# A two-layer network under a list scheduler: who takes a cast, four blocks to a value group, half-width levels

## The chip, the cores and the metric

The kernel runs on one core of a Trainium2 chip. The core has a matrix engine (TensorE, PE in the profile; its weight loads are listed apart as PEld), a vector engine (VectorE, DVE), a scalar engine (ScalarE, ACT), a general-purpose engine (GpSimd, POOL), and an engine that issues most of the DMA transfers here (SyncE, SP). The metric is device time in microseconds for one execution of the whole program.

## The reference

The reference is a small two-layer network in f32 over a sequence of 1024 tokens with width 1024. Layer 0 mixes tokens with sliding-window attention with sinks, layer 1 with a gated linear recurrence (HGRN2); each layer ends with an MLP with a squared ReLU. Cut to what matters:

```python
for layer in range(DEPTH):                       # DEPTH = 2
    h = rmsnorm(x, mix_norm[layer])
    if layer % 2 == 0:
        # 16 query heads, 4 key/value heads of 64, window 128, blocks of 128 tokens
        qkv = h @ w_qkv + b_qkv                   # rotary on q and k
        scores = einsum(q_block, [k_prev, k_own]) * HEAD_DIM ** -0.5   # masked to the window
        e = exp(scores - m); probs = e / (sum(e) + exp(sink - m))
        y = einsum(probs, [v_prev, v_own]) @ w_o
    else:
        q, f, i, g = split(h @ w_in, 4)           # 8 heads of 128, chunks of 64 tokens
        forget = lb + (1 - lb) * sigmoid(f); k = 1 - forget
        # per chunk, from the state and within the chunk with the decay between s and t
        o = (q * exp(b)) @ state + tril((q_t . decay(t, s) . k_s)) @ i
        y = (rmsnorm(o) * silu(g)) @ w_o
    x = x + y
    x = x + square(relu(rmsnorm(x) @ w_up)) @ w_down   # d_ff = 4096
return rmsnorm(x, final_norm)
```

## The kernel before

Activations are kept as tiles of 128 x 512 in f32. A large product is built from three products in the format fp32r, because one such product is not exact enough: each operand is split into a high part (a cast to fp32r) and a low part (the operand minus the high part). `mm3` issues high x high, high x low and low x high. `weight_split` makes the parts of a weight tile: `wh` is the high part, a cast, and `wl` the low part, a subtraction on DVE. `split` does the same to activations (tiles `a`, `t`). The MLPs go through a Strassen scheme with seven products, so sums of weights (`m`, `a`) are split too.

The stages follow one another and overlap at their seams. The first 80 us are the first half of the q, k, v projection; until about 290 the attention blocks run between the second half of it and the first half of the output projection; then the output projection ends (to 340). The first MLP's up projection takes 340 to 640, its down projection 640 to 930. From 960 to 1440 the recurrence runs for eight heads, with the projections of the gates between, and 1440 to 1545 is its output projection. The second MLP is 1545 to 1830 and 1830 to 2140.

**What sets the order.** Every operation is first recorded (`Net.op`, `copy`, `tt`, `mm`) with the engine or engines that can do it and an estimated cost; `Schedule.order` then makes a list schedule: it always serves the engine that is free first in its own estimate, and there takes the ready operation of the lowest rank. `issue` emits the operations in that order, so all instructions in the profile carry the line of its inner function, L333, and one has to go by the names of the tiles. Each engine runs its queue in this order on the chip.

Only one kind of operation has two engines to choose from: the casts that `copy` records with `("ACT", "DVE")`. When an engine would take such a cast, `better_elsewhere` asks whether the other engine, after what stands ahead there, would end it sooner; if so the engine leaves it and takes another. The recorded cost of a cast is lower on DVE than on ACT; recorded costs only steer the order.

**Attention.** `attend` handles, for each half of the sequence (four blocks of 128 tokens) and each key/value head, the blocks in turn. `attend_block` makes the scores (two PSUM buffers of the kind `q`), the masked softmax in an `m` tile, the transposed probabilities (one more `q` buffer) and two `t` tiles with what the values are multiplied by. After every two blocks `values` multiplies them in the column form of PE, which puts two products of 64 output rows beside one another in the array, into one `q` buffer, and copies the result out. There are four `q` and four `p` buffers of PSUM, 18 `t` tiles and 60 `a` tiles.

**Recurrence.** Inside a chunk of 64 tokens the scores are built in levels, so that the decay between two tokens can be put into the two factors. For level `lg` with half width H = 2^lg all 64 x 64 scores of all chunks are computed (16 products of 64 output rows in the column form, two records each in the trace), and a masked copy (`copy_predicated`) takes from them those where the later token is in the second half of a block of 2H and the earlier one in the first. Level -1 is the diagonal, and a last product covers pairs of chunks.

Of the kernel before, what the change touches and what calls it, by code (L numbers as in the profile page):

```python
# [17 lines left out]
P = 128  # L18
# [4 lines left out]
TH = T // NH  # L23
# [8 lines left out]
HD = 64  # L32
ROT = 16
NBLK = T // P
BPH = NBLK // NH
# [6 lines left out]
CH = 64  # L42
# [88 lines left out]
    "Pool": {"SP": 200.0, "PE": 190.0, "ACT": 75.0, "DVE": 74.0, "Pool": 102.0},  # L131
}
WEIGH = 1.0
DRAIN = {"whole": 120.0, "columns": 120.0}
LEAD = 100
WARM = 8
# [4 lines left out]
class Schedule:  # L141
# [42 lines left out]
    def order(self):  # L184
        free_at, pending, ready, done, form = {}, {}, {}, [], None
# [25 lines left out]
        def better_elsewhere(op, e, t):  # L211
            waiting = sum(o.ways[e][1] for _, o in ready[e] if not o.engine and len(o.ways) == 1)
            for other, (_, cost) in op.ways.items():
                if other != e:
                    ahead = sum(o.ways[other][1] for r, o in ready.get(other, ()) if r < op.rank and not o.engine)
                    if max(t, free_at.get(other, 0.0)) + ahead + cost < t + op.ways[e][1] + WEIGH * waiting:
                        return True
            return False

        while True:  # L220
            best = None
            for e in ENGINES:
                p, r = pending.setdefault(e, []), ready.setdefault(e, [])
                t = free_at.get(e, 0.0)
# [4 lines left out]
                if not r:  # L229
                    if not p:  # L230
                        continue
                    t = max(t, p[0][0])
# [4 lines left out]
            t, e = best  # L237
            p, r = pending[e], ready[e]
            while p and p[0][0] <= t:
                _, rank, op = heapq.heappop(p)  # L240
                heapq.heappush(r, (rank, op))
            left, op = [], None
            while r and op is None:
                rank, o = heapq.heappop(r)
                if o.engine:
                    continue
                if len(o.ways) > 1 and better_elsewhere(o, e, t):
                    left.append((rank, o))
                else:
                    op = o  # L250
# [6 lines left out]
            if op.form and op.form != form:  # L257
                form, t = op.form, t + DRAIN[op.form]
            free_at[e] = t + cost
# [19 lines left out]
class Net:  # L279
# [635 lines left out]
    def attend(self, hf, out):  # L915

        blocks = range(hf * BPH, hf * BPH + BPH)
        for gp in range(NG // 2):
            stacks = [[None] * 4 for _ in range(2)]
            for j in range(4):  # L920
                pq = self.psum("q")
                for n in blocks:
                    c = slice((n % BPH) * P, (n % BPH) * P + P)
                    self.transpose(pq[:, c], self.q[n][gp][:, j * P : j * P + P])
                for e in range(2):
                    r, o = self.rows(e)
                    s = self.a(F32R)
                    self.act(s[r], pq[r], AF.Copy, scale=HD**-0.5)
                    self.stt(s[o], pq[r], HD**-0.5, s[r].bitcast(F32), ALU.mult, ALU.subtract)
                    stacks[e][j] = s  # L930
            for e in range(2):
                g = 2 * gp + e
                for j in range(2):
                    out[g, j] = self.a()
                for n in blocks[::2]:
                    parts = []
                    for b in (n, n + 1):
                        parts.append(self.attend_block(g, b, stacks[e]))
                        yield
                    self.values(g, n, parts, out)  # L940

    def values(self, g, n, parts, out):

        tok = slice((n % BPH) * P, (n % BPH) * P + 2 * P)
        both = [y for block in parts for y, v in block]
        po = self.psum("q").rearrange("p (h s) -> p h s", h=2)
        for b, block in enumerate(parts):
            for k, (y, v) in enumerate(block):
                for rr in range(2):
                    self.mm(po[rr * HD : rr * HD + HD, :, b * P : b * P + P], v, y[:, 2 * rr : 2 * rr + 2],  # L950
                            k == 0, k == len(block) - 1, 2 * P, 2.0, "columns", both)
        for j in range(2):
            self.copy(out[g, j][:, tok].only(n), po[:, j], 2 * P)

    def attend_block(self, g, n, stacks):
        i = (n >= 3) + (n >= 6)
# [184 lines left out]
    def recurrence(self, e, gates, totals, out):  # L1141

        nc = self.nc
        NC = NH * BPH
        chunk = lambda z, j: z[:, j * CH : j * CH + CH]
        scores = self.t(F32, (P, NC, CH))
        tots, tot = [self.t(tag="m") for _ in range(NH)], [g[1] for g in gates]
        at = 0
        for lg in range(-1, LEVELS):
            part = self.psum("q").rearrange("p (c t) -> p c t", c=NC)  # L1150
            both = [z for q, f, k, g, v in gates for z in (q, k)]
            for hf, (q, f, k, g, v) in enumerate(gates):
                for c in range(BPH):
                    for b in range(2):
                        rows = slice(b * CH, b * CH + CH)
                        j = 2 * c + b
                        self.mm(part[rows, hf * BPH + c], chunk(k, j), chunk(q, j), True, True, CH, 2.06, "columns", both)
            if lg < 0:
                mask = self.diag.unsqueeze(1).to_broadcast([P, NC, CH])
                self.tt("DVE", scores, part, mask, ALU.mult)  # L1160
                for q, f, k, g, v in gates:
                    self.tt("any", q, q, f, ALU.mult)
                yield
                continue
            mask = self.level_mask[lg].unsqueeze(1).to_broadcast([P, NC, CH])
            self.op("DVE", nc.vector.copy_predicated, [scores], [mask, part], 70 + TH * 1.04, scores, mask, part)
            at, tot = self.double(1 << lg, gates, tot, tots, at)
            yield
        cross = self.psum("q")[:CH].rearrange("p (c t) -> p c t", c=NC)
        both = [z for q, f, k, g, v in gates for z in (q, k)]  # L1170
# [4 lines left out]
        for hf in range(NH):  # L1175
            s, c = self.t(F32, (P, BPH, 2, CH)), slice(hf * BPH, hf * BPH + BPH)
# [9 lines left out]
        for hf, (q, f, k, g, v) in enumerate(gates):  # L1186
            s = weights[hf]
# [34 lines left out]
            y = self.split(g, self.t if keep else None)  # L1222
# [169 lines left out]
```

## Time and profile before

| | |
|---|---|
| runs | 2169.42, 2171.11, 2174.44 us (median 2171.11) |
| the profiled execution | 2174.92 us, of which the span from first to last instruction is 2173.1 |
| mean granted clock of PE | 0.994 |
| busy: PE, DVE, ACT, POOL | 2136.3, 1818.1, 848.0, 61.2 us |
| DMA | 316.50 MB, mean 146 GB/s |

PE's products of 128 x 512 are its common unit; in the up projection of the first MLP 1307 PE records take 300 us. Busy times by stage:

| stretch (us) | what runs | PE | DVE | ACT |
|---|---|---|---|---|
| 0 to 80 | q, k, v, first half | 76.79 | 67.63 | 41.38 |
| 80 to 160 | attention | 76.39 | 70.71 | 50.66 |
| 160 to 240 | attention | 79.40 | 71.47 | 58.13 |
| 240 to 292 | end of attention | 47.45 | 48.66 | 44.89 |
| 640 to 930 | first MLP, down | 288.39 | 254.09 | 112.00 |
| 960 to 1060 | first gates | 98.85 | 94.10 | 50.65 |
| 1060 to 1440 | recurrence | 378.41 | 333.71 | 131.01 |
| 1830 to 2140 | second MLP, down | 307.12 | 269.92 | 124.08 |

How the rows of the profile are read: a row of the timeline has its start and its duration in us, the engine, the operation with output<-inputs (buffer numbers left out), its shape, the count of instructions drawn together, and in brackets how long the engine had stood idle before it and what ended that. A row of the waits has the waiting engine and tile, what it waited for, the sum in us, the number of times and the longest. A row of the table of stretches has the stretch, its length, the busy time of PE, PEld, DVE, ACT and POOL with counts, PE's granted clock, the share of DMA and GB/s. A row of groups has the count of instructions, their busy time in us, the mean of one in ns, and the engine's idle time before them with what ended most of it.

### The profile page before, as it was taken

The page shows a single profiled execution, that of the slowest core. Times are in us where ns is not written, and L with a number is a line of the kernel's source. Part 1 is how long each engine was busy: PE and PEld are TensorE (multiplying, and loading weights), DVE is VectorE, ACT ScalarE, POOL GpSimd, SP SyncE. Part 2 cuts the span into 40 slices and gives each one's busy share as a digit, 9 for nine tenths or more (in the row PEclk, how much of TensorE's full clock was granted, in tenths as well). Part 3 has the DMA queues.
Part 4 walks back from the last instruction along what each step waited for, and adds up shares of the span by engine and source line. Part 5 has one row for each costly group of instructions (what it writes and reads, how often), then busy time and mean ns, then how long its engine had stood idle before and what let it go on. Part 6 is the DMA issues. An engine that isn't in the chain of part 4 may idle for free.

```text
span 2173.1 us, 32411 instructions
## 1 busy us (share of the span) xinstructions
PE 2136.3 (98%) x11464; PEld 1723.3 (79%) x11464; DVE 1818.1 (84%) x3544; ACT 848.0 (39%) x1778; POOL 61.2 (3%) x121
## 2 busy tenths in 40 slices
PE   9999999999999999999999999999999999999998
PEld 7777778888887888877788888778788887888787
DVE  8899889767779888899998988878876678988886
ACT  5567755122134224465333333343421223422444
POOL 4030000000000000000100000000000000000000
PEclk9999999999999999999999999999999999999999
DMA  6212353333369767731111111547333336976652
GB/s 207 76 44 87 118 193 112 105 104 116 103 213 309 261 210 233 250 126 54 59 58 56 59 55 59 193 148 221 98 112 107 107 113 219 304 250 218 209 180 78
DMA packets 174274, 316.50 MB, mean 146 GB/s; under 512 B 19616, under 2 KB 21664, under 8 KB 174112
## 3 DMA queue, kind: packets, MB, share of 16 engines
q1 hardware_dynamic: 174112, 314.43, 44.7%
q8 instruction: 90, 1.47, 0.3%
q14 instruction: 72, 0.59, 0.1%
HBM read 250.39 MB, written 63.96 MB: 145 GB/s over the span
## 4 chain that ended last, share of the span: by engine, by line
PE 86%; DVE 7%; ACT 3%; issue 2%; DMA 2%; SPq 0%; POOL 0%; POOLq 0%; DVEq 0%; ACTq 0%
PE q L333 48%; PE p L333 38%; DVE a L333 3%; DVE t L333 2%; ACT a L333 1%; DVE wl L333 1%; DMA wr<-in_down 1%; DVE m L333 1%; ACT t L333 1%; DMA wr<-in_wqkv 0%; ACT wh L333 0%; ACT m L333 0%; DMA a<-in_x 0%; DVE wh L333 0%; SPq L333 0%
## 5 line engine op out<-in xcount | busy, mean ns | idle before, releaser
L333 PE MATMUL q<-a,wh 128*128 128x512 f32 x2560 | 799.9, 395 | 8.1 <-DVE t L333 3.4
L333 PE MATMUL p<-a,wh 128*128 128x512 f32 x2336 | 754.0, 401 | 6.1 <-ACT wh L333 3.4
L333 PEld LDWEIGHTS q<-a,wh 128*128 128x128 f32 x2560 | 481.1, 188 | 122.6 <-ACT t L333 4.3
L333 PEld LDWEIGHTS p<-a,wh 128*128 128x128 f32 x2336 | 431.7, 189 | 105.3 <-ACT wh L333 4.3
L333 PE MATMUL q<-a,wl 128*128 128x512 f32 x1280 | 500.3, 394 | 0.0
L333 PE MATMUL p<-a,wl 128*128 128x512 f32 x1168 | 462.3, 396 | 0.1
L333 PEld LDWEIGHTS q<-a,wl 128*128 128x128 f32 x1280 | 240.9, 188 | 56.9
L333 PEld LDWEIGHTS p<-a,wl 128*128 128x128 f32 x1168 | 220.3, 189 | 49.7 <-DVE wl L333 0.6
L333 DVE TENSOR_TENSOR wl<-wr,wh 128x512 fp32r<-128x512 f32 x352 | 240.9, 686 | 14.4 <-ACT wh L333 4.2
L333 ACT COPY t<-q 128x512 f32<-128x512 f32 (+2 forms) x201 | 111.7, 562 | 361.8 <-PE q L333 353.1
L333 DVE TENSOR_TENSOR a<-t,a 128x512 fp32r<-128x512 f32 (+1 forms) x294 | 194.7, 685 | 0.5 <-DMA t<-d 0.2
L333 DVE TENSOR_TENSOR wl<-m,wh 128x512 fp32r<-128x512 f32 x256 | 176.4, 690 | 15.5 <-ACT wh L333 6.7
L333 DVE CAST wh<-wr 128x512 fp32r<-128x512 f32 x202 | 86.2, 427 | 120.7 <-PE p L333 74.1
L333 ACT CAST wh<-m 128x512 fp32r<-128x512 f32 x154 | 95.9, 623 | 217.1 <-PE q L333 149.9
L333 DVE TENSOR_TENSOR t<-t,t 128x512 f32<-128x512 f32 (+3 forms) x265 | 157.5, 612 | 21.2 <-DMA t<-d 14.2
L333 ACT CAST a<-t 128x512 fp32r<-128x512 f32 x191 | 115.5, 618 | 127.0 <-PE q L333 82.5
L333 ACT CAST wh<-wr 128x512 fp32r<-128x512 f32 x150 | 92.7, 619 | 178.5 <-PE p L333 113.1
L333 DVE TENSOR_TENSOR m<-wr,wr 128x512 f32<-128x512 f32 x160 | 109.6, 688 | 24.9 <-DMA wr<-in_up 12.1
L333 PE MATMUL p<-wh,a 128*128 128x512 f32 x384 | 128.2, 402 | 0.9 <-ACT wh L333 0.7
L333 PEld LDWEIGHTS q<-t,t 128*64 128x64 f32 (+1 forms) x2160 | 98.0, 144 | 25.1 <-PE p L333 12.4
L333 PE MATMUL q<-t,t 128*64 128x64 f32 (+1 forms) x2160 | 112.8, 231 | 0.0
L333 DVE CAST wh<-m 128x512 fp32r<-128x512 f32 x102 | 43.9, 430 | 74.4 <-PE q L333 61.4
(118 smaller groups left out, 2133.5 us busy)
## 6 DMA issues: line engine op xcount, KB each, us to landing
t<-d SPq DMA_DIRECT2D x296, 256.0 KB, 4.6
wr<-in_down SPq DMA_DIRECT2D x256, 256.0 KB, 4.0
d<-t SPq DMA_DIRECT2D x180, 256.0 KB, 2.6
wr<-in_up SPq DMA_DIRECT2D x128, 256.0 KB, 3.0
wr<-in_win SPq DMA_DIRECT2D x68, 256.0 KB, 2.9
a<-d SPq DMA_DIRECT2D x60, 256.0 KB, 4.5
wr<-in_wqkv SPq DMA_DIRECT2D x48, 256.0 KB, 3.0
d<-a SPq DMA_DIRECT2D x48, 256.0 KB, 2.6
```

Of the source, the lines that this page charges most:

```text
L333: fn(*[place(a) for a in args], **{k: place(v) for k, v in kw.items()})
```

## The change

Three things are edited.

- `better_elsewhere` adds `SPARE` = 1000 ns to DVE's side of the comparison. DVE takes a cast only if ACT would end it more than 1 us later than DVE could.
- `attend` collects four blocks instead of two before it calls `values`, which now fills two `q` buffers in one stay in the column form. There are 8 such groups instead of 16; the products and the copies are the same in number and size.
- In `recurrence` the levels from 0 up compute only the columns of the later halves: `later` picks the second half of each block of 2H, so a product has 32 moving columns instead of 64, and the masked copy works on 256 elements for each partition instead of 512, with source, mask and target picked with strides. Level -1 and the last product stay.

```diff
+SPARE = 1000.0
...
-                    if max(t, free_at.get(other, 0.0)) + ahead + cost < t + op.ways[e][1] + WEIGH * waiting:
+                    spare = SPARE if e == "DVE" else 0.0
+                    if max(t, free_at.get(other, 0.0)) + ahead + cost < t + op.ways[e][1] + WEIGH * waiting + spare:
                         return True
...
-                for n in blocks[::2]:
+                for n in blocks[::4]:
                     parts = []
-                    for b in (n, n + 1):
+                    for b in range(n, n + 4):
                         parts.append(self.attend_block(g, b, stacks[e]))
                         yield
                     self.values(g, n, parts, out)
...
-        po = self.psum("q").rearrange("p (h s) -> p h s", h=2)
+        po = [self.psum("q").rearrange("p (h s) -> p h s", h=2) for _ in range(2)]
...
-                    self.mm(po[rr * HD : rr * HD + HD, :, b * P : b * P + P], v, y[:, 2 * rr : 2 * rr + 2],
+                    self.mm(po[b // 2][rr * HD : rr * HD + HD, :, b % 2 * P : b % 2 * P + P], v, y[:, 2 * rr : 2 * rr + 2],
                             k == 0, k == len(block) - 1, 2 * P, 2.0, "columns", both)
-        for j in range(2):
-            self.copy(out[g, j][:, tok].only(n), po[:, j], 2 * P)
+        for b in range(2):
+            for j in range(2):
+                self.copy(out[g, j][:, b * 2 * P : b * 2 * P + 2 * P].only(n + 2 * b), po[b][:, j], 2 * P)
...
-            part = self.psum("q").rearrange("p (c t) -> p c t", c=NC)
+            H = 1 << max(lg, 0)
+            n, width = (1, CH) if lg < 0 else (CH // (2 * H), CH // 2)
+            part = self.psum("q")[:, : NC * width].rearrange("p (c t) -> p c t", c=NC)
+            later = lambda z: z if lg < 0 else z.rearrange("p (n a h) -> p n a h", a=2, h=H)[:, :, 1]
...
-                        self.mm(part[rows, hf * BPH + c], chunk(k, j), chunk(q, j), True, True, CH, 2.06, "columns", both)
+                        self.mm(part[rows, hf * BPH + c], chunk(k, j), later(chunk(q, j)), True, True, CH, 2.06, "columns", both)
...
-            mask = self.level_mask[lg].unsqueeze(1).to_broadcast([P, NC, CH])
-            self.op("DVE", nc.vector.copy_predicated, [scores], [mask, part], 70 + TH * 1.04, scores, mask, part)
+            mask = later(self.level_mask[lg]).unsqueeze(1).to_broadcast([P, NC, n, H])
+            target = scores.rearrange("p c (n a h) -> p c n a h", a=2, h=H)[:, :, :, 1]
+            part = part.rearrange("p c (n h) -> p c n h", n=n)
+            self.op("DVE", nc.vector.copy_predicated, [target], [mask, part], 70 + NC * width * 1.04, target, mask, part)
```

Since all operations go through the list schedule, the edit moves instructions in the whole program. Of the 379 casts that DVE had it keeps 19, and ACT has 1034 instead of 674. Three places follow, each with an engine's rows before and after. A name has the tile's number and, behind the underscore, the value's number; the second differs between the two programs.

The first is ACT at the end of the first MLP's down projection, where the output of the MLP is normalized and the first weights for the next stage are split. Before:

```order
L333 ACTIVATE t2491_9696<-a2245_8785 128x512
L333 CAST wh2401_9702<-a1744_7052 128x512
L333 CAST wh2413_9706<-a1776_7171 128x512
L333 CAST wh2419_9710<-a1792_7229 128x512
L333 CAST a2482_9712<-t2481_9471 128x512
L333 ACTIVATE t2492_9716<-a2247_8795 128x512
L333 CAST wh2395_9720<-a1728_6988 128x512
L333 ACTIVATE t2532_9740<-a2129_8453,c01_91 128x512
```

After:

```order
L335 CAST a2437_9539<-a1840_7411 128x512
L335 ACTIVATE t2485_9543<-a2349_9170 128x512
L335 ACTIVATE t2457_9551<-a2351_9176,c01_91 128x512
L335 ACTIVATE t2486_9557<-a2351_9176 128x512
L335 CAST wh2395_9564<-a1728_6990 128x512
L335 CAST a2439_9573<-t2435_9159 128x512
L335 CAST a2445_9579<-t2441_9225 128x512
L335 ACTIVATE t2461_9584<-a2353_9182,c01_91 128x512
```

The high part wh2395 now stands directly behind the activation t2486, a square of a residual tile. Before, t2486 stands at row 698 of ACT's queue and wh2395 at row 725, behind wh2401, wh2413 and wh2419.

The second is ACT at the end of the recurrence's output projection, where the squares of the residual (t3716 to t3722) and the high parts of normalized input tiles stand between the casts of weights. Before:

```order
L333 ACTIVATE t3720_15968<-a3638_15778 128x512
L333 ACTIVATE t3721_15974<-a3648_15836 128x512
L333 ACTIVATE t3722_15977<-a3658_15907 128x512
L333 CAST wh3780_15980<-wr3772_15756 128x512
L333 CAST a3707_15983<-t3706_15848 128x512
L333 CAST a3710_15989<-t3709_15858 128x512
L333 CAST a3713_15993<-t3712_15869 128x512
L333 CAST a3685_15997<-t3684_15913 128x512
L333 COPY t3760_16001<-q3757_15885 128x512
L333 COPY t3761_16003<-q3758_15946 128x512
```

After:

```order
L335 ACTIVATE t3720_15961<-a3638_15775 128x512
L335 CAST a3701_15967<-t3671_15676 128x512
L335 ACTIVATE t3721_15971<-a3648_15834 128x512
L335 ACTIVATE t3722_15977<-a3658_15899 128x512
L335 CAST a3704_15981<-t3703_15788 128x512
L335 CAST wh3780_15984<-wr3772_15748 128x512
L335 COPY t3760_15988<-q3757_15883 128x512
L335 CAST a3699_15993<-t3667_15619 128x512
L335 CAST a3707_15999<-t3706_15845 128x512
L335 COPY t3761_16003<-q3758_15944 128x512
```

The copy t3760, which empties a PSUM buffer, moved directly behind wh3780; before, four casts of activations stand between. Ahead of wh3780 there are more casts than before (wh3755 and a3701, a3704 among the squares).

The third is DVE at the start of the first MLP's down projection, between the scaled squares t1603 and t1607 of the activation function; t1607 reads a PSUM buffer and thereby sets it free, and a1687 is a sum of activations that ACT casts next. Before:

```order
L333 SCALAR_TENSOR_TENSOR t1603_6731<-t1599_6686 128x512
L333 TENSOR_TENSOR m1673_6736<-wr1674_6692,wr1675_6702 128x512
L333 TENSOR_TENSOR a1686_6742<-t1682_6598,a1685_6654 128x512
L333 TENSOR_TENSOR a1680_6754<-m1673_6736,wr1665_6671 128x512
L333 TENSOR_TENSOR t1598_6646<-t1598_6646,t1600_6752 128x512
L333 TENSOR_TENSOR wl1645_6769<-m1641_6540,wh1644_6746 128x512
L333 SCALAR_TENSOR_TENSOR t1605_6776<-t1598_6646 128x512
L333 TENSOR_TENSOR a1687_6782<-t1688_6609,t1682_6598 128x512
L333 TENSOR_TENSOR a1702_6787<-t1698_6621,a1701_6668 128x512
L333 TENSOR_TENSOR a1703_6797<-t1704_6629,t1698_6621 128x512
L333 TENSOR_TENSOR a1695_6807<-a1687_6782,a1694_6792 128x512
L333 SCALAR_TENSOR_TENSOR t1607_6805<-q1594_6509,t1607_6805 128x512
```

After:

```order
L335 SCALAR_TENSOR_TENSOR t1603_6733<-t1599_6686 128x512
L335 TENSOR_TENSOR a1664_6740<-m1657_6706,wr1649_6562 128x512
L335 TENSOR_TENSOR a1687_6746<-t1688_6607,t1682_6595 128x512
L335 TENSOR_TENSOR a1702_6756<-t1698_6616,a1701_6670 128x512
L335 TENSOR_TENSOR t1598_6650<-t1598_6650,t1600_6754 128x512
L335 TENSOR_TENSOR wl1645_6773<-m1641_6547,wh1644_6763 128x512
L335 SCALAR_TENSOR_TENSOR t1605_6778<-t1598_6650 128x512
L335 TENSOR_TENSOR m1673_6784<-wr1674_6720,wr1675_6730 128x512
L335 TENSOR_TENSOR a1695_6791<-a1687_6746,a1694_6768 128x512
L335 TENSOR_TENSOR a1680_6797<-m1673_6784,wr1665_6668 128x512
L335 TENSOR_TENSOR a1703_6807<-t1704_6626,t1698_6616 128x512
L335 SCALAR_TENSOR_TENSOR t1607_6805<-q1594_6507,t1607_6805 128x512
```

The sum a1687 moved from seven rows behind t1603 to two; the weight sum m1673 moved behind t1605. Ten rows stand between t1603 and t1607 in both.

More of the change, by code (lines that the diff above doesn't have):

```diff
@@ L942, in values @@
     def values(self, g, n, parts, out):
-        tok = slice((n % BPH) * P, (n % BPH) * P + 2 * P)
         both = [y for block in parts for y, v in block]
-        po = self.psum("q").rearrange("p (h s) -> p h s", h=2)
+        po = [self.psum("q").rearrange("p (h s) -> p h s", h=2) for _ in range(2)]
         for b, block in enumerate(parts):
```

## The prediction

> **What bounds the kernel now.** I read the page's first part, then the table of stretches, then PE's waits, then the timeline around each of the longer ones.
>
> ```profile
> PE 2136.3 (98%) x11464; PEld 1723.3 (79%) x11464; DVE 1818.1 (84%) x3544; ACT 848.0 (39%) x1778; POOL 61.2 (3%) x121
> ...
> 240.00:292.00 52.00, 47.45 (x288) 35.38 (x289) 48.66 (x97) 44.89 (x135) 0.45 (x2) 0.97 0.54 176
> 340.00:640.00 300.00, 299.96 (x1307) 243.10 (x1306) 222.26 (x379) 72.92 (x131) 0.00 (x0) 1.00 0.38 119
> 930.00:960.00 30.00, 26.76 (x114) 21.48 (x113) 26.87 (x75) 16.90 (x32) 0.36 (x2) 0.94 0.38 117
> 1440.00:1545.00 105.00, 99.94 (x438) 80.71 (x437) 92.33 (x172) 50.90 (x90) 0.00 (x0) 0.95 0.58 184
> ```
>
> PE is busy 98% of the span, and in the first up projection (340:640) it has no gap at all, with DVE at 74% and ACT at 24%; the second reads the same. There nothing that is moved between DVE and ACT can shorten the kernel. What is left is 2173.1 - 2136.3 = 36.8 us in which PE stands still, and the time that a lowered clock costs: (1 - clock) x length is 1.6 us in 240:292, 1.8 in 930:960, 5.2 in 1440:1545. These three seams between stages are also where DVE is busiest (94%, 90%, 88%). Who keeps PE waiting:
>
> ```profile
> PE q L333 <- DVE t L333: 5.2, 6, 1.7
> PE q L333 <- DVE m L333: 5.0, 6, 3.2
> PE q L333 <- ACT t L333: 4.9, 5, 1.8
> PE p L333 <- ACT wh L333: 4.1, 3, 3.2
> PE q L333 <- DVE a L333: 2.4, 4, 1.6
> ```
>
> These five make 21.6 us, in 24 waits. So the prize of a better order is some 22 us plus slow clock, and the change must be priced wait by wait.
>
> **The casts.** The new rule leaves 19 of 379 casts on DVE and sends 360 to ACT.
>
> ```profile
> L333 DVE CAST wh<-wr 128x512 fp32r<-128x512 f32 x202 | 86.2, 427 | 120.7 <-PE p L333 74.1
> L333 DVE CAST wh<-m 128x512 fp32r<-128x512 f32 x102 | 43.9, 430 | 74.4 <-PE q L333 61.4
> L333 ACT CAST wh<-wr 128x512 fp32r<-128x512 f32 x150 | 92.7, 619 | 178.5 <-PE p L333 113.1
> ```
>
> Each takes about 0.43 us from DVE and 0.62 us on ACT: DVE loses 360 x 0.427 = 154 us (84% to 77%), ACT gains 223 us (39% to 49%). The idle time ahead of these casts on both engines was ended mostly by PE (it gives buffers back), so in the steady stages the cast waits for PE and not the reverse. The 0.19 us by which a cast gets longer is covered by that lead, and I cost it at nothing there, as I do the gain. If that cover were gone, every pair of MLP weights would pay; the rows at 340:640 with ACT at 24% say it has room. The casts therefore count only at the seams, below.
>
> **The masked copies.**
>
> ```profile
> L333 DVE COPY_PREDICATED t<-c,q 128x512 f32<-128x512 int32 x48 | 35.2, 734 | 9.2 <-PE q L333 8.3
> L333 DVE COPY_PREDICATED m<-c,q 128x256 f32<-128x256 int32 x56 | 23.7, 444 | 0.2
> ```
>
> 48 copies over half the elements: 48 x (0.734 - 0.444) = 13.9 us of DVE, in the recurrence, where PE is the bound. On the path: nothing. The new source and target are strided, which no row shows; bounds for one copy are 0.44 and the old 0.73 us, and either is hidden.
>
> **The halved level products.** 48 groups of 16 products, 32 records each, go from 64 to 32 moving columns.
>
> ```profile
> 998.99 0.95 PE L333 MATMUL q<-c,t 128*128 128x1 f32 x8
> 1004.88 1.05 PE L333 MATMUL q<-c,c 128*128 128x128 f32 x8
> 1073.70 1.15 PE L333 MATMUL q<-t,t 128*64 128x64 f32 x32
> ```
>
> The first two rows decide: eight products with one moving column take 0.95 us, eight with 128 take 1.05. With 128 times fewer columns the series loses 0.10 us, which is the end of its last product; the step between products is set by the load of the weights. The level's weights stay 64 columns wide, so its step should stay, and only the tail shrinks: 0.10 x 32/128 = 0.025 us, x 48 = 1.2 us. If the moving columns set the step after all (the series of 32 in 1.15 us would fall to half at best), the gain is 48 x 0.57 = 27 us; that is the upper bound and a rival. I take -1.2, nearest the one-column row. The Trainium skill has a rule for each: "TensorE: Matmul & The Clock Gate", section Back-to-back issue gap, makes the gap grow with the moving columns over 2.4 GHz, which is the gain; its section LDWEIGHTS makes a load cost its columns over 1.2 GHz, an estimated 53 ns for 64, which is none. The two rows side with the second.
>
> **The value groups.** Sixteen become eight, so PE enters and leaves the column form eight times less.
>
> ```profile
> 277.90 0.40 PE L333 MATMUL p<-a,wl 128*128 128x512 f32 x1
> 278.23 1.95 PE L333 MATMUL q<-t,a 128*64 128x256 f32 x16
> ```
>
> The group begins 0.33 us after a product that elsewhere is followed in 0.23 us (340:640 has 1307 records in 300 us), so entering costs 0.10 us; leaving I put at the same. 8 x 0.2 = -1.6 us; between 0.8 and 1.6. What the larger groups hold longer is under the rivals.
>
> **The seams, one by one.**
>
> Start. The first weight cast goes from DVE to ACT, into the queue that also scales the inputs.
>
> ```profile
> 4.27 0.63 DVE L333 CAST wh<-wr 128x512 fp32r<-128x512 f32 x1 [2.80 <-DMA wr<-in_wqkv]
> 4.43 0.72 ACT L333 ACTIVATE a<-a,c 128x512 fp32r<-128x512 f32 x1 [0.34 <-DMA c<-in_par]
> 5.21 0.80 PE L333 MATMUL p<-wh,a 128*128 128x512 f32 x1 [0.22 <-ACT a L333]
> 9.77 0.49 PE L333 MATMUL p<-wh,a 128*128 128x512 f32 x1 [0.65 <-ACT wh L333]
> ```
>
> Behind that activation and two small ones the cast ends near 5.9, not 4.9: the first product moves from 5.21 to about 6.1. The second set of weights (9.77) is cast behind one more input's two activations and comes about 1.8 later, but then finds its low half ready. Between +0.9 and +2.5, taken +1.2, near the first.
>
> End of attention.
>
> ```profile
> 285.18 0.63 PE L333 MATMUL q<-c,m 128*128 128x128 f32 x4 [3.23 <-DVE m L333]
> 286.45 3.26 PE L333 MATMUL q<-t,a 128*64 128x256 f32 x16
> 290.24 0.53 PE L333 MATMUL p<-a,wh 128*128 128x512 f32 x1 [0.53 <-DVE a L333]
> ```
>
> PE waits 3.2 us for a softmax block on DVE, and the value group behind it runs at the slow clock (3.26 us against 1.95): 3.23 + 1.31 + 0.53 = 5.1 us. In the new order DVE does the output projection's low halves far earlier, ahead of the last blocks, so PE has other products there, and four-odd us of casts are off DVE. But the softmax chain itself runs some blocks later. From 0 to -5.1, I take -3.
>
> Two waits of the down projections, of one kind.
>
> ```profile
> 654.85 0.73 PE L333 MATMUL q<-a,wh 128*128 128x512 f32 x2 [1.61 <-DVE t L333]
> 1847.56 0.73 PE L333 MATMUL q<-a,wh 128*128 128x512 f32 x2 [1.74 <-DVE t L333]
> ...
> 2023.50 0.73 PE L333 MATMUL q<-a,wh 128*128 128x512 f32 x2 [1.14 <-ACT t L333]
> 652.42 0.62 ACT L333 CAST a<-a 128x512 fp32r<-128x512 f32 x1 [1.62 <-DVE a L333]
> ```
>
> PE waits for DVE to read a PSUM buffer, DVE for a relu on ACT, and ACT stood 1.62 us in front of a cast of a DVE sum. In the new order that sum is five rows nearer to t1603 on DVE, 5 x 0.6 us, which more than ends ACT's wait; but then DVE's own ten rows set the time. About half goes: -0.8 each, -1.6 (0 to -3.3). At 2023.50 the copy that releases PE no longer stands behind a cast: -1.1 (0 to -1.1).
>
> Into the recurrence.
>
> ```profile
> 937.82 0.60 ACT L333 CAST wh<-a 128x512 fp32r<-128x512 f32 x1
> 938.48 1.76 PE L333 MATMUL p<-a,wh 128*128 128x512 f32 x4 [3.24 <-ACT wh L333]
> 950.00:960.00 10.00, 10.00 (x50) 8.29 (x49) 6.87 (x16) 2.07 (x4) 0.00 (x0) 1.00 0.61 206
> 965.00:990.00 25.00, 24.40 (x108) 18.91 (x107) 24.96 (x42) 19.39 (x36) 0.00 (x0) 1.00 0.08 31
> ```
>
> PE waits 3.24 us for wh2395 and then loses 1.8 us to the clock. The cast is needed first of its set and stands last; before, it stood 27 rows behind the activation t2486, in the new order it stands right behind it, and this wait goes. Late next is DVE: from 965 to 990 it is full, and PE, 5 us earlier, would catch up with it. What DVE can make good is its idle time, 10.00 - 6.87 = 3.1 us in 950:960. So -3 of 5 (0 to -5).
>
> Small waits in the recurrence.
>
> ```profile
> 1066.49 0.49 PE L333 MATMUL q<-t,m 128*128 128x128 f32 x2 [0.57 <-DVE m L333]
> ```
>
> Two or three like this one; DVE casts that stood ahead of what PE waits for are gone: -1 (0 to -1.5).
>
> Into the second MLP.
>
> ```profile
> 1530.64 0.60 ACT L333 CAST wh<-wr 128x512 fp32r<-128x512 f32 x1
> 1533.23 1.05 ACT L333 COPY t<-q 128x512 f32<-128x512 f32 x2
> 1531.30 0.73 PE L333 MATMUL q<-a,wh 128*128 128x512 f32 x2 [1.74 <-ACT wh L333]
> 1533.86 1.22 PE L333 MATMUL q<-a,wh 128*128 128x512 f32 x2 [1.83 <-ACT t L333]
> ```
>
> Two waits, 1.74 for wh3780 and 1.83 for a copy behind four more casts, then slow clock. In the new order two or three more ACT rows stand ahead of wh3780 (+0.9), and the copy follows it at once (the second wait gone, -1.8; clock up to -2.3). -2, between +0.9 and -3.2. The clock is the uncertain part: here 1.74 and 1.83 us of standing, with three products between, set off the slow stretch. The Trainium skill, "TensorE: Matmul & The Clock Gate", section What's actually happening, says a window of 3.4 us judged idle halves the clock; by it one wait of 2.6 us could escape or not, an estimated 2 us either way.
>
> New waits. ACT is at 44.89 of 52 us in 240:292 and now takes nine more casts there, 5.6 us. It would be at 97%. For waits behind it I add +3 (0 to +8).
>
> Sum: -1.2 -1.6 +1.2 -3 -1.6 -1.1 -3 -1 -2 +3 = -10.3 us, and 0 for the rest. The profiled execution took 2174.92 us (span 2173.1), 3.8 above the median of the runs, 2171.11; against that median the sum gives 2160.8.
>
> **Rivals.** Levels at half the step: 27 us more, about 2135. For it: 32 records in 1.15 us are also what 64 columns would take at the pace of the 16 records of 256 in 1.95. Against it: the one-column row. Chance 0.06.
>
> The waits only move: PE meets DVE or ACT a little later at each seam (965 to 990 is the example), what the seams gave comes back, and what stays is -1.2 -1.6 and little else: about 2168.5. For it: DVE is full on both sides of 950:960. Against it: DVE gets 154 us back overall. Chance 0.18.
>
> Slower: attention is starved by the four-block group. Each of the eight groups now needs the probabilities of four blocks before its products start, holds two of the four q buffers of PSUM, and the next blocks' scores need two more; and the casts that fed PE's other work now stand in ACT's queue between the exponentials. If a group makes PE wait 2.5 us (the 3.23 us at 285.18 is such a wait), 8 x 2.5 = +20, less the 10: about 2181. It ends slower from (10.3 + 4.3)/8 = 1.8 us a group. For it: ACT near full in 240:292. Against it: PE's other products (the projection) stand between the groups. Chance 0.19.
>
> **Numbers.** This kernel's measurement can tell about 0.2%, 4.3 us. My forecast, 2160.8, has 0.57; with the first rival faster comes to 0.63. The second rival is within 0.2% for most of its chance: 0.17. Slower 0.20. The forecast's own terms reach from 2150 to 2168; the range to 2176 takes in the second rival and the nearer part of the third, and leaves out the first below and the rest above.
>
> **What would show it.** Right: DVE near 1650 us and ACT near 1070; PE's busy time down by only 1 to 3 us in the stretch of the recurrence, and 32 level records still in about 1.1 us; no wait of 3 us near 935 and 282; one wait, not two, near 1530; first product near 6.1. Wrong: level series under 0.8 us; waits of PE on ACT a, wh or on DVE m of over 1.8 us at several value groups between 80 and 290; DVE as releaser of PE between 960 and 990 by several us.

## The result

The changed kernel takes as long as the one before. Over 13 runs of each on the same chip the medians are 2171.04 and 2171.69 us; the ratio is 0.9995 with a 95% interval of 0.9982 to 1.0008. The forecast was 2160.8 us, 10.3 below.

The profiled execution of the changed kernel took 2170.39 us. Its page, its waits of PE, and the stretches that were shown of before:

```profile
PE 2132.4 (98%) x11464; PEld 1721.8 (79%) x11464; DVE 1668.6 (77%) x3184; ACT 1040.7 (48%) x2138; POOL 58.1 (3%) x121
...
240.00:292.00 52.00, 50.35 (x317) 39.20 (x317) 44.84 (x89) 44.17 (x133) 1.02 (x3) 1.00 0.36 120
340.00:640.00 300.00, 299.97 (x1306) 243.09 (x1306) 193.51 (x310) 111.49 (x199) 0.00 (x0) 1.00 0.39 124
930.00:960.00 30.00, 29.34 (x131) 23.68 (x130) 29.13 (x80) 16.57 (x31) 0.18 (x1) 1.00 0.46 149
960.00:1060.00 100.00, 96.69 (x633) 77.35 (x633) 89.34 (x178) 52.54 (x100) 1.01 (x3) 0.98 0.18 53
```

```profile
PE p L335 <- ACT wh L335: 6.8, 4, 2.8
PE q L335 <- ACT t L335: 4.6, 10, 1.3
PE q L335 <- DVE wl L335: 4.2, 2, 2.3
PE q L335 <- ACT wh L335: 2.4, 1, 2.4
```

DVE and ACT moved as forecast (near 1650 and 1070 us expected, 1668.6 and 1040.7 found), and the steady stages are untouched: 340:640 has no gap before and none now. But the list of PE's waits has not become shorter. The row DVE t went from 5.2 us to 0.6, DVE m from 5.0 to 1.7; in their place stand ACT wh, with 9.2 us in two rows against 5.8 before, and a releaser that hardly appeared before, DVE wl, with 4.2 us.

Where the time went is best seen by taking the same product of PE in both traces and subtracting its start times (the median over 16 neighbours; worked out from the traces, profiled execution against profiled execution). A step is what a stretch added to the changed kernel's delay:

| stretch (us of before) | step, us | what is there |
|---|---|---|
| 0 to 20 | +3.2 | second weights at 11.82 instead of 9.77, then slow clock |
| 20 to 340 | -7.0 | attention and output projection |
| 640 to 660, 1830 to 1850 | -0.9, -1.1 | the wait behind the relu |
| 740 to 760 | +2.1 | new wait on DVE wl |
| 930 to 945 | -4.1 | the wait for wh2395 is gone |
| 975 to 990 | +3.6 | new wait for wh2643 |
| 1060 to 1400 | +1.5 | recurrence |
| 1400 to 1455 | -3.1 | a wait at 1450 and slow clock behind it are gone |
| 1525 to 1560 | -1.7 | one wait of 2.4 us instead of two |
| 1920 to 2000 | +4.0 | new wait on DVE wl, then slow clock |
| 2000 to 2030 | -1.4 | the wait on the copy is gone |
| all else | +0.9 | |
| sum | -4.0 | |

In single executions the gains are 19 us and the losses 15; a profile of one execution each shows -4, the medians of 13 hardly any. The profiled execution of before (2174.92 us) lies 3.2 us above the median of its runs and that of the changed kernel 0.7 below, so the -4 is these two executions rather than the change. The gain at 1400 to 1455 is in no term of the prediction; it is this wait of before, with slow clock behind it:

```profile
1450.75 1.14 PE L333 MATMUL p<-a,wh 128*128 128x512 f32 x2 [1.06 <-DVE t L333]
```

The new waits, as the timeline of the changed kernel has them:

```profile
11.82 1.88 PE L335 MATMUL p<-wh,a 128*128 128x512 f32 x4 [2.76 <-ACT wh L335]
...
746.77 0.50 PE L335 MATMUL q<-a,wl 128*128 128x512 f32 x1 [1.81 <-DVE wl L335]
...
980.19 0.73 PE L335 MATMUL p<-a,wh 128*128 128x512 f32 x2 [2.38 <-ACT wh L335]
...
1937.36 0.79 PE L335 MATMUL q<-a,wl 128*128 128x512 f32 x1 [2.34 <-DVE wl L335]
```

And the two operations of the recurrence that were sized by neighbouring rows:

```profile
1074.17 1.13 PE L335 MATMUL q<-t,t 128*64 128x32 f32 x32
...
L335 DVE COPY_PREDICATED t<-c,q 128x256 f32<-128x256 int32 x48 | 25.8, 538 | 27.6 <-PE q L335 26.9
```

A level goes from 1.15 to 1.13 us with half the moving columns; in both traces its records come in pairs that start 58 ns apart. The masked copy with strides takes 538 ns, between the bounds of 444 and 734.

### The profile page after: what moved, and what is told of

It reads as the page before. It is cut to its first block, busy times and chain, and to the rows that moved or that the text cites. A ratio compares the mean times of both kernels' runs of the same rounds, so it can differ in the third digit from the quotient of the medians.

```text
span 2168.6 us, 32427 instructions
## 1 busy us (share of the span) xinstructions
PE 2132.4 (98%) x11464; PEld 1721.8 (79%) x11464; DVE 1668.6 (77%) x3184; ACT 1040.7 (48%) x2138; POOL 58.1 (3%) x121
## 5 line engine op out<-in xcount | busy, mean ns | idle before, releaser
L335 ACT CAST wh<-wr 128x512 fp32r<-128x512 f32 x345 | 212.7, 619 | 250.3 <-PE p L335 147.7
L335 ACT CAST wh<-m 128x512 fp32r<-128x512 f32 x256 | 159.2, 623 | 322.6 <-PE q L335 243.6
L335 ACT CAST a<-t 128x512 fp32r<-128x512 f32 x208 | 126.8, 618 | 81.0 <-PE q L335 45.7
L335 ACT CAST a<-a 128x512 fp32r<-128x512 f32 x119 | 73.5, 622 | 102.9 <-DVE a L335 54.5
L335 PE MATMUL q<-t,t 128*64 128x32 f32 (+2 forms) x2160 | 111.6, 230 | 0.0
L335 DVE TENSOR_TENSOR t<-p,t 128x512 f32<-128x512 f32 x96 | 65.7, 687 | 55.8 <-PE p L335 54.9
```

What stands on the lines that cost most here:

```text
L335: fn(*[place(a) for a in args], **{k: place(v) for k, v in kw.items()})
```

## The experiments

Each is timed against the kernel before on the same chip. Where medians of two experiments are compared, they can come from two chips; the ratios then say more.

### One part at a time

The rule for the casts alone:

```diff
+SPARE = 1000.0
...
-                    if max(t, free_at.get(other, 0.0)) + ahead + cost < t + op.ways[e][1] + WEIGH * waiting:
+                    if max(t, free_at.get(other, 0.0)) + ahead + cost < t + op.ways[e][1] + WEIGH * waiting + (SPARE if e == "DVE" else 0.0):
```

> Only the rule for the casts; groups of two blocks and full levels as before. Theory (the rule moves the waits of PE, gains and losses both): every seam reads as in the changed kernel, that is first product near 6.0 us and the second weights near 11.8, a wait of PE on a low half near 745 and near 1935 of about 2 us each, no wait of 3 us near 935 but one of 2 to 2.6 us near 978, small waits on ACT t in each head of the recurrence; time within 2 us of the changed kernel, 0 to +3 us against it. Rival (the larger value groups hold the gain in attention): the end of attention keeps its wait of about 3 us near 282, and the time is 4 to 7 us above the changed kernel.

The changed kernel with the rule switched off:

```diff
-SPARE = 1000.0
+SPARE = 0.0
```

> The changed kernel with SPARE 0: four-block groups and halved levels alone, casts as before (366 on DVE). Theory: start, 745, 1935 and the recurrence read as before (first product 5.2, second weights 9.8, no wait on a low half in the down projections, a wait of 3 us near 935); time 0 to 4 us below the kernel before, from the groups (1.6) and the levels (1.2). Rival (groups of four starve PE in attention): waits of 1.8 us and more at value groups between 80 and 290, time 5 us or more above the kernel before.

The kernel before with the new `recurrence` alone, and with the new `attend` and `values` alone; the edits are those of the change, shown here in part:

```diff
+            later = lambda z: z if lg < 0 else z.rearrange("p (n a h) -> p n a h", a=2, h=H)[:, :, 1]
...
-                        self.mm(part[rows, hf * BPH + c], chunk(k, j), chunk(q, j), True, True, CH, 2.06, "columns", both)
+                        self.mm(part[rows, hf * BPH + c], chunk(k, j), later(chunk(q, j)), True, True, CH, 2.06, "columns", both)
```

> Only the halved levels. Theory (the load of the weights sets the step): a series of 32 records goes from 1.15 to 1.12 us, 48 series give -1.2 us and the waits stay where they were; 1 us below the kernel before, not to be told from it. Rival (moving columns set the step): series near 0.6 us, 20 us and more below.

```diff
-                for n in blocks[::2]:
+                for n in blocks[::4]:
```

> Only the four-block groups. Theory: the form is entered and left eight times less, -1.6 us, and attention's other waits change by less than 3 us either way; total between -4 and +2 us against the kernel before. Rival (starved attention): waits of 1.8 us and more at the groups, +5 us or more.

Measured, as the ratio to the kernel before with its 95% interval:

| kernel | median us | ratio |
|---|---|---|
| all three parts (the change) | 2171.04 | 0.9995 [0.9982, 1.0008] |
| rule alone | 2174.67 | 1.001 [1.0, 1.002] |
| groups and levels, no rule | 2165.13 | 0.9972 [0.9962, 0.9983] |
| levels alone | 2170.30 | 0.9994 [0.9985, 1.0002] |
| groups alone | 2168.05 | 0.9981 [0.9971, 0.9991] |

So the two parts that were priced at 1.2 and 1.6 us give some 6 us together, and the rule, which was to give the rest, takes them away again. The groups alone are worth 0.19%, some 4 us. The levels alone cannot be told from nothing; in their trace each 50 us of the recurrence get 0.14 us shorter, 0.9 us from 1060 to 1400, which fits 1.2 us in all.

The rule alone has the waits that the theory named, in the same places, and one of them is worse than in the changed kernel:

```profile
749.27 0.79 PE L334 MATMUL q<-a,wl 128*128 128x512 f32 x1 [3.72 <-DVE wl L334]
...
1944.62 0.50 PE L334 MATMUL q<-a,wl 128*128 128x512 f32 x1 [2.06 <-DVE wl L334]
```

Its median is 3.6 us above the changed kernel's, outside the 0 to 3 us expected and short of the 4 to 7 us of the rival. At the end of attention PE still waits, now for ACT, and the clock from 240 to 292 us is 0.97 as before:

```profile
282.47 0.63 PE L334 MATMUL q<-c,m 128*128 128x128 f32 x4 [2.38 <-ACT t L334]
```

The groups alone, with nearly all casts where they were, shorten the wait at the end of attention from 3.23 us to 1.24 and take the slow clock behind it away; a wait of 1.70 us follows for a low half:

```profile
287.92 0.63 PE L333 MATMUL q<-c,m 128*128 128x128 f32 x4 [1.24 <-DVE m L333]
...
294.51 0.50 PE L333 MATMUL p<-a,wl 128*128 128x512 f32 x1 [1.70 <-DVE wl L333]
```

The changed kernel has 1.35 us there, for DVE m. From 80 to 340 us the groups alone gain 5.8 us, the rule alone 3.0, the whole change 7.0. What a larger group saves by itself can be read from its rows, two groups of before and one of the changed kernel:

```profile
101.10 1.52 PE L333 MATMUL q<-t,a 128*64 128x256 f32 x12
112.01 1.95 PE L333 MATMUL q<-t,a 128*64 128x256 f32 x16
...
112.82 3.24 PE L335 MATMUL q<-t,a 128*64 128x256 f32 x28
```

The two take 3.47 us, the one 3.24; 0.23 us less, eight times, is 1.8 us. In the traces of the change, of the groups alone and of groups with levels PE stands 1.8 us or more at no value group between 80 and 290: the rival of a starved attention is out.

### The low half that stands behind a transfer

At 745 the queue of DVE in the changed kernel reads:

```profile
742.63 0.68 DVE L335 TENSOR_TENSOR wl<-a,wh 128x512 fp32r<-128x512 f32 x1
745.42 0.69 DVE L335 TENSOR_TENSOR t<-t,t 128x512 f32<-128x512 f32 x1 [2.12 <-DMA t<-d]
746.03 0.68 DVE L335 TENSOR_TENSOR wl<-a,wh 128x512 fp32r<-128x512 f32 x1
```

The second row is t2065, the difference of two stored activations that come back by DMA; the third is wl1898, for which PE waits. DVE stands 2.12 us in front of t2065 for its transfer, while all that wl1898 needs has long been there (its high part left ACT at 737.6). Before, wl1898 stood five rows ahead of t2065. With the cast of its high part on ACT, behind eight copies that empty PSUM at the change of pass, the list schedule puts wl1898 one row behind t2065. Two experiments touch this place. One asks for the stored activations earlier:

```diff
         z = self.t()
+        self.s.lead = 150
         self.dma(z, self.hid[p + i * MT // 2, hf], 4 * P * TH)
+        self.s.lead = 0
```

> The changed kernel with the loads of the stored activations of the down projection ranked 150 operations earlier, so that t2066 and t2067 are asked for earlier and t2065 stands 12 rows ahead of wl1898. Theory (DVE stands in front of t2065 for its transfer, with wl1898 behind it): the wait on DVE wl near 745 and 1935 goes or falls under 0.5 us, 2 to 6 us below the changed kernel, unless the earlier loads take buffers from other transfers. Rival (wl1898 is late because its high part is late on ACT, behind eight copies): the waits stay at 2 us.

The other keeps more casts on DVE:

```diff
-SPARE = 1000.0
+SPARE = 500.0
```

> The changed kernel with SPARE 500 instead of 1000: DVE keeps 230 casts, among them the first of the start, and at the change of pass in the down projections wl1898 stands five rows ahead of the sum t2065 again. Theory (the rule loses its time where a cast moves behind other work of ACT and a low half then stands behind something that waits): the waits near 745 and 1935 are gone (2 and 4 us), the first product is near 5.3 us; the wait near 978 stays, since m2638 still stands directly ahead of the split block's last sums; 4 to 8 us below the changed kernel. Rival (the new waits come from transfers that vary from run to run): waits of 2 us on DVE wl near 745 and 1935 here too, time within 2 us of the changed kernel.

The earlier loads bring 2165.62 us, 0.9968 [0.9957, 0.998] of the kernel before, 5.4 us below the changed kernel's median. What is left of the row DVE wl for the buffers q is:

```profile
PE q L335 <- DVE wl L335: 0.2, 1, 0.2
```

The spread of the runs is smaller too: 2163.83 to 2166.59 over five runs, where the changed kernel had 2167.48 to 2179.03 over thirteen; with the new rank of the section on the seam, each over twelve runs, it is 2162.62 to 2169.22 with the earlier loads and 2161.03 to 2179.63 without.

The other traces agree on this cause. The steps against before, at 740 to 760 and at 1920 to 2000 us, with the kernels of the sections below taken in, are:

| kernels | 740 to 760, us | 1920 to 2000, us |
|---|---|---|
| SPARE 1000, loads as before: the change, the rule alone, seam, start | +2.1, +6.8, +4.6, +4.6 | +4.0, +3.9, -0.1, +1.9 |
| SPARE 1000, earlier loads: alone, recurrence, seam | all under 0.1 | all under 0.1 |
| no rule: levels, groups, both, both with earlier loads | 0.0, +0.1, +0.1, +0.1 | 0.0, -0.2, 0.0, 0.0 |

In all four kernels of the first row t2065 stands directly ahead of wl1898. So the row also shows that what such a place costs differs from one execution to the next. Whether the earlier loads gain something of their own was tried with the rule off:

```diff
-SPARE = 1000.0
+SPARE = 0.0
...
+        self.s.lead = 150
         self.dma(z, self.hid[p + i * MT // 2, hf], 4 * P * TH)
+        self.s.lead = 0
```

> SPARE 0 with four-block groups, halved levels and the earlier loads of the stored activations. Theory (the earlier loads only take away the wait on a low half that the rule made): no such wait was there, so the time stays within 1.5 us of the run with SPARE 0 alone (2165). Rival (the earlier loads gain by themselves): 3 us or more below it.

It has 2165.07 us (0.9967 [0.9957, 0.9978]) against 2165.13 without the earlier loads. They gain nothing by themselves; with the rule they gain what these waits cost.

SPARE 500 missed its expectation: 2172.09 us (0.9996 [0.9985, 1.0007]). The wait at 745 is gone and the one at 1935 down to 0.92 us, but from 240 to 292 it is 3.1 us slower than the changed kernel, with a wait for another low half:

```profile
287.49 0.79 PE L335 MATMUL p<-a,wl 128*128 128x512 f32 x1 [3.22 <-DVE wl L335]
```

No transfer is in front of this one; DVE is busy without a gap from 273 us until it has made it. The profiled execution (2167.72 us) is the fastest of the twelve runs, so the trace need not show what the others lose, and why SPARE 500 is not faster stays in part open.

### The recurrence

```diff
+        self.s.spare = 0.0
         for e in range(KT):
...
         run(before)
+        self.s.spare = SPARE
```

Here each operation keeps the SPARE that held when it was recorded, so the rule is off for the eight heads of the recurrence and the gates between; the earlier loads are in.

> The changed kernel with the earlier loads, and SPARE 0 for what is recorded in the recurrence and its gates. Theory (in the recurrence the rule puts the scaling t2880 ahead of t2874 and the copy t2852 in ACT's queue, 0.6 us a head): the small waits on ACT t at 1124, 1180 and so on are gone, the recurrence is 3 us shorter than in the changed kernel, the time 2 to 3.5 us below the run with the earlier loads alone (2165.6), 2162 to 2164. Rival (these waits cost nothing, being covered elsewhere): the same time as that run.

The time is 2159.77 us, 0.9951 [0.9939, 0.9963], 0.5% below the kernel before. By the medians it is 5.9 us below the earlier loads alone; by the ratios, 0.9951 against 0.9968, it is 3.7 us with intervals that touch, so whether it is more than the 2 to 3.5 us expected is not settled. Waits of PE from 1060 to 1400, first in the changed kernel, whose row the earlier loads alone have too, then here:

```profile
PE q L335 <- ACT t L335: 1.6, 6, 0.3
```

```profile
PE q L336 <- ACT t L336: 0.4, 1, 0.4
```

Product against product with the earlier loads alone, five heads in a row are 0.61 to 0.63 us shorter each, 3.1 us in all, as said. The rest of the difference is 2.8 us at 1830 to 1850, where the trace of the earlier loads alone has a wait of 1.81 us (on ACT t) and slow clock behind it, and this one a wait of 0.56; with one profile each that is not settled. In ACT's queue the activation t2880, which waits for DVE, stood ahead of t2874 and of the copy t2852 that PE's next products need; with the rule off there, t2874 is ahead of it again.

This kernel, with the rule everywhere but in the recurrence, is also 5.3 us below the one with the earlier loads and no rule at all (2165.07 us, timed with it on the same chip; by the ratios 3.5, and the intervals touch). So the rule does gain something where these two costs are taken off.

### The seam into the recurrence

```diff
     def strassen_weights(self, first, second, done=()):
-        self.s.lead = LEAD
+        self.s.lead = 130
```

> The changed kernel with the operations on weights of the seven-product scheme ranked 130 instead of 100 operations earlier; m2638 then stands 43 rows ahead of a2584 instead of 3. Theory (the wait near 978 is for wh2643, whose input m2638 is queued behind the split of activations on DVE): that wait goes; 2 to 4 us below the changed kernel, less what DVE, full from 960 to 985, then makes late in the split block. Rival (DVE's work as a whole sets the time there): PE waits as long for an activation (DVE a or t) within 20 us, time the same.

> The changed kernel with the earlier loads and the weights of the seven-product scheme ranked 130 ahead. Theory (DVE's whole work between 960 and 1005 sets the time, so an earlier m2638 only moves the wait): within 1.5 us of the run with the earlier loads alone (2165.6), the wait near 978 replaced by one of 2 us or more before 1005. Rival (the wait for wh2643 is the cost): 3 us or more below that run.

The second kernel has the earlier loads as well. Times: 2170.92 us (0.9992 [0.9976, 1.0008]) and, with the earlier loads, 2164.22 (0.9969 [0.996, 0.9979]) against 2165.62 without the new rank. The wait near 978 is gone, worth 5.2 us by 990, and all but 0.2 of it is lost again by 1010 (5.2 and 0.2 in the other pair):

```profile
991.94 0.73 PE L335 MATMUL p<-a,wh 128*128 128x512 f32 x2 [0.81 <-ACT wh L335]
993.95 1.05 PE L335 MATMUL q<-c,t 128*128 128x1 f32 x8 [1.28 <-DVE t L335]
```

So an earlier m2638 only moves the wait, as the rival had it, which fits DVE as what holds this seam. In the changed kernel it is busy 25.00 of 25 us around the wait, and with the new rank 25.00 as well:

```profile
960.00:985.00 25.00, 22.11 (x92) 17.39 (x92) 25.00 (x43) 17.89 (x33) 0.00 (x0) 0.93 0.12 42
```

### The start

```diff
-                w = self.weight_split(ahead[kt] if known else self.raw(self.io["wqkv"][cg, kt // 2][:, c : c + TH]))
+                w = self.weight_split(ahead[kt] if known else self.raw(self.io["wqkv"][cg, kt // 2][:, c : c + TH]), ("DVE",) if known and kt < 2 else ("ACT", "DVE"))
```

> The changed kernel with the first two casts of weights pinned to DVE. Theory (the cast behind the scaling of the inputs on ACT delays the second weights): first product near 5.2 us, second weights near 9.8, the drift of the start is back: 1 to 4 us below the changed kernel, by how late the third input's transfer lands. Rival (the transfers set the start): the second weights near 11.8 as before, time the same.

With the first two casts on DVE the kernel is not faster: 2174.17 us, 1.0012 [1.0002, 1.0022], where 1 to 4 us below the changed kernel were expected. In the traces the second weights follow the landing of the third input tile, which differs by up to 2 us between executions with the same rows ahead of it. In the changed kernel, and with the earlier loads, ACT's activation for that tile starts at:

```profile
10.02 0.72 ACT L335 ACTIVATE a<-a,c 128x512 fp32r<-128x512 f32 x1 [2.73 <-DMA a<-in_x]
```

```profile
8.06 0.73 ACT L335 ACTIVATE a<-a,c 128x512 fp32r<-128x512 f32 x1 [0.17 <-DMA a<-in_x]
```

In the second of these the start is 3.5 us shorter than in the first, and as long as before, although every queue has the same rows there. Most of the +3.2 us of the table is the transfer's, not the cast's. Over the six traces in which the rule has moved the first cast, the step from 0 to 80 us is -0.35 to +3.19, in the mean +1.4; in the four without the rule the mean is -0.1.

## Why the prediction was wrong

The forecast of a clear gain failed, since the term "new waits" was put in the wrong place and every gain at a seam was priced apart from the waits that the same move makes. With the groups and levels in, the rule was to gain and costs 5.9 us (2171.04 against 2165.13; 5.0 by the ratios): low halves wait behind a transfer at the change of pass, and ACT's queue is in a worse order in the recurrence. Point by point:

- **What bounds the kernel** was right: PE, with some 22 us of waits as the whole prize. In the up projections the moved casts cost nothing and gained nothing, as said. But the three seams named as those where DVE is busiest leave one out: from 960 to 1060 it is busy 94.10 of 100 us, and a new wait came there.
- **Levels** (-1.2) and **masked copies** (0 on the path): right. The rival of a step set by the moving columns is refuted by 1.13 us for a series. The Trainium skill, "TensorE: Matmul & The Clock Gate", section LDWEIGHTS, gives an estimated 53 ns for 64 weight columns, and the trace agrees with pairs 58 ns apart for 64 and for 32 moving columns. Its section Back-to-back issue gap gives the formula that the prediction names only for a single product by itself; for a stream of weight loads and products it says that both set the spacing, so it promises no gain here either.
- **Value groups** (-1.6): the size was right, 1.8 us by the rows. **End of attention** (-3): the owner was wrong. The groups alone give 4 us, among them most of the end of attention, which was credited to the casts taken from DVE; with the rule alone the wait there is 2.38 us, behind ACT. A wait of this kind is what the +3 was added for; it came with the rule alone, and in the change, which has the groups too, 0.74 us for ACT a is left of it.
- **Into the recurrence** (-3): wrong, and by the mechanism of the second rival. The wait at 938 went, the one at 980 came; -4.1 and +3.6. "What DVE can make good is its idle time" was the step that failed: DVE was full, it finished the split of activations, which the order now put ahead of m2638 (43 rows ahead of a2584 before, 3 after), and PE needed the weights.
- **Recurrence** (-1): wrong in sign. The rule costs 0.6 us a head, 3 us, through the order of ACT's queue, which the prediction does not look at there; ACT is idle two thirds of the time. PE's busy time from 1060 to 1440 fell by 0.5 us, not by 1 to 3.
- **New waits** (+3, at ACT near 290): the size was too small and the place another. The waits on DVE wl at the change of pass of both down projections took 2.1 and 4.0 us in one execution, 6.8 and 3.9 in the profile of the rule alone. The forecast had put these stages at nothing, as covered by the lead of the casts; that holds for the pairs in the middle, not for the first weights behind eight PSUM copies.
- **Start** (+1.2): 3.2 in the profile, but this is a transfer that varies; the mean of six traces, +1.4, is near it.
- **Into the second MLP** (-2): -1.7 in the profile, near by luck. There is one wait instead of two, as said, but with the same products in the same order it is 2.41 us long here and 3.20 with the earlier loads, where the step is -1.0; and the levels alone, whose rows there are those of before, have -0.5. **Relu waits** (-1.6): -2.0 in the profile; **2023** (-1.1): -1.4. But with the levels alone, whose order there is the same as before row for row, the wait at 2023 is absent too and the one near 655 costs 2.3 us more. These single waits are not the order's alone, and a term for each from one profile was more than the profile can carry.
- **The range**: the terms' own upper bounds add up to +9.4 us, 2180.5, and not to 2168; the measured time lies well inside what the prediction itself held possible.
- **The signs**: nearly all that were to show the forecast right came (DVE, ACT, 1.13 us for a level, no wait of 3 us near 935 and 282, one long wait near 1530, first product at 5.98), and none of those for wrong, yet the time did not fall. They watched the waits that were priced, not the places where new ones came.

Of the rivals, "the waits only move" (2168.5 us, chance 0.18) is the one that came, with 2171.04. Its mechanism is shown at the seam into the recurrence; the waits at the change of pass and in the recurrence were in no rival.

## What to carry to other kernels

In a list-scheduled kernel with in-order queues, a cheaper engine choice is not paid where the operation runs but where its result queues: behind what does the low half, the copy, the activation now stand, and does that one wait for a transfer? Look for it at the change of a pass, where copies pile up on one engine, and not in the steady middle, which was covered here. And before pricing a wait from one profile, ask whether another execution of the same order has it.

## What was not expected of the hardware

- Executions of the same order differ by single waits in PE's stream: the same rows have 8.06 and 10.02 us for the landing of an input, and the wait of PE near 655 is 1.61 us in the kernel before and 2.34 us with slow clock behind it in the kernel with the levels alone, whose rows up to there are the same:

```profile
655.65 0.83 PE L333 MATMUL q<-a,wh 128*128 128x512 f32 x2 [2.34 <-DVE t L333]
```

- A wait of about 2 us can cost some 1.7 us more when the granted clock drops behind it: behind the 2.34 us at 1937 it is 0.50 for 3.4 us, and the step there is 4.0; from 960 to 985 it is 0.93, 1.75 us of 25. The drop does not follow from the wait's length alone: in the profiles it comes behind the 1.06 us at 1450 in the kernel before and not behind the 1.81 us at 746 in the changed one.
- A masked copy of 256 elements that reads and writes with strides takes 538 ns, contiguous 445.
- With the rule, DVE's own idle time has a new owner: it stands 150 us for high parts from ACT, of which little reaches PE, whose waits for a low half are 4.7 us in all.

```profile
DVE wl L335 <- ACT wh L335: 150.1, 113, 4.3
```
